# Gathered expert rows beside the first half: 2.2 per weight unit, and weights split two units ahead

## The chip, the cores and the metric

The kernel runs on one core of a Trainium2 chip. The metric is the device time of one execution in microseconds (us). TensorE (PE in the rows), VectorE (DVE), ScalarE (ACT), GpSimd (POOL) and the DMA queues of SyncE (SP) each work through their own list of instructions in order, and wait for one another by semaphores.

## What is computed

One decoder block on 512 tokens of width 1024 in f32: an adaLN-modulated RMSNorm, retention and a causal gMLP side by side, merged by sigmoid gates, one output projection, and then a PEER expert layer, which is what the change is about. Each token picks 16 experts for each of 8 heads out of 16,384 (two top-16 searches over 128 keys and a third over their sums), and needs one row of 1024 values from each of two tables for each of its 128 picks:

```
expert = k1 * PEER_N_KEYS + k2
g = jax.nn.softmax(top_s, axis=-1)
ue = expert_u[expert]                       # 128 rows of 1024 for each token
act = jax.nn.gelu(jnp.einsum('td,thkd->thk', hb, ue), approximate=False) * g
ve = expert_v[expert]
return jnp.einsum('thk,thkd->td', act, ve)
```

## The kernel before

**Tiles and stages.** The 512 tokens are four tiles of 128. Tile 0 goes through the block alone and first, and its experts are known early. The other three tiles follow together. For tiles 0 and 3 the expert layer is done by gathering; for tiles 1 and 2 by dense matmuls over all 16,384 experts, with a matrix of one-hot weights.

**Table rows.** A gathered "row" is, for one pick j, one expert's 1024 f32 values for each of the 128 tokens of a tile: an indirect DMA on POOL's queue (`gather`, L934) into a 128x1024 buffer. `consume` then does one VectorE instruction with it: for table `u` a product with the tile's activations, summed into a dot (L950); for table `v` a multiple added to an accumulator (L955). There are 512 rows: 128 of `u` and 128 of `v` for tile 0, then the same for tile 3. They are consumed in this order, in three places:
- beside the three tiles' first half, by `bg_gather`, which is called after each weight unit. A credit `cr` grows by `GB1` for each unit (by 0.6 while the seven jobs in `tq` last, that finish tile 0's search); each whole credit consumes a row and issues the next gather. Only `u` rows of tile 0 can be done here, 128 at most.
- in the query and experts-ahead phases, at fixed steps of a list that `plan` makes;
- in the final loop, where `gathers(n)` spreads whatever is left over the loop's items, in proportion to their cost.

**Weight units.** `Stream` feeds TensorE with weights in units of 128x1024. A unit is loaded by SP into a `raw` buffer (five), and, unless it is used plain, split into a high part `wh` by a ScalarE copy (L87) and a low part `wl` by a VectorE subtraction (L90). `wh` and `wl` have four buffers each. `get` returns unit k; ahead of that it issues loads as far as `ra` = 5 units, and splits as far as `sa` units (k included). Three matmuls use the parts: wh with the high activations, wl with the high, wh with the low. Gathered rows have their own buffers (two `ga`, one `gt`, later two more `gt`), and take in turns one buffer of the `wh` ring and one of the `wl` ring (`gfree += ["wh", "wl"]`); in the ring a buffer that was free longest is taken.

**The stages on which rows below are cut.** In the first half `gemm` runs 14 groups of four units: up (two groups, with gMLP mixing beside them), gate-b (two), gMLP out (two), v and g (four, with the retention's scores, products and norm beside them), gate-a (two), retention out (two). Each group ends in evictions. Then come the output projection (eight units, each raw unit scaled by a gate on VectorE, L344), the query phase (16 units, with the search for tiles 1 to 3 on VectorE), the experts-ahead phase (plain units of `uT`, L1355), and the final loop over 128 items (L1681), which loads `v`, and `uT` for the experts that weren't done ahead, splits half of the `v` units and those `uT` units, and makes the weights `aw` (L1654) and their low part `ah` (L1665) on VectorE, with the loop's gathered rows in between. Time is that of one execution from first to last instruction, and nothing is scheduled at run time: the order on each engine is that of the program.

Of the kernel before, what the change touches and what calls it, by code (L numbers as in the profile page):

```python
# [36 lines left out]
TO = 16  # L37
GSC = 2.0 ** 14
GPU = 1.4
GB1 = 1.4  # L40
VN = 2
LA = 2
PRE = 6
# [147 lines left out]
def block_kernel(ctx: ExitStack, tc: tile.TileContext, a, out, dbg=None):  # L191
# [116 lines left out]
    ws = Stream(nc, wt)  # L308
# [629 lines left out]
    def gather_all():  # L938
        while gfree and ng[0] < lim[0]:
            gather()  # L940

    def consume():
        i = ng[1]
        ng[1] += 1
        r, b = gt_t.pop(i)
        if not dropped(b):
            gfree.append(b)
        j, G = i % NJ, GT[i // (2 * NJ)]
        if i // NJ % 2 == 0:
            V.scalar_tensor_tensor(r, r, 1.0, G.h, op0=OP.mult, op1=OP.mult, accum_out=G.dots[:, j:j + 1])  # L950
            if j == NJ - 1:
                A.activation(G.dots, G.dots, AF.Gelu)
                V.tensor_tensor(G.dots, G.dots, G.g, op=OP.mult)
        else:
            V.scalar_tensor_tensor(G.acc, r, G.dots[:, j:j + 1], G.acc, op0=OP.mult, op1=OP.add)  # L955
# [21 lines left out]
    tq = []  # L977
# [34 lines left out]
    gfree += ga  # L1012
    gfree.append(t0_tile("gt"))
    gfree += ["wh", "wl"]
    ws.sa = 2
    cr = [0.0]

    def bg_gather():
        if tq:
            tq.pop(0)()  # L1020
        cr[0] = min(cr[0] + (0.6 if tq else GB1), 4.0)
        gather_all()
        while cr[0] >= 1.0 and ng[1] < ng[0]:
            cr[0] -= 1.0
            consume()
            gather_all()
# [235 lines left out]
    def xn2_tile(t):  # L1262
        rsqrt(kp, rs2[:, t:t + 1], ss2[:, t:t + 1], 1, 1.0 / D, "r2")
        V.tensor_scalar(xn2[:, t, 0:512], x2[:, t, 0:512], rs2[:, t:t + 1], None, op0=OP.mult)
        A.activation(xn2[:, t, 512:1024], x2[:, t, 512:1024], AF.Copy, scale=rs2[:, t:t + 1])
# [45 lines left out]
    for t in range(NA):  # L1311
# [6 lines left out]
        else:  # L1318
# [3 lines left out]
            ws.split(ws.ng + 2)  # L1322
            x2_tile(t + 1)
            xn2_tile(t + 1)
    ws.sa = 2
    gdrop[:] = []
    gfree += ["wh", "wl"]

# [586 lines left out]
```

## Time and profile before

| | |
|---|---|
| median of three runs | 1793.97 us (1792.15 to 1796.37) |
| profiled execution | 1793.85 us |
| its span, first to last instruction | 1791.9 us |
| instructions | 22,168 |
| busy: PE, DVE, ACT, POOL | 1590.3, 1412.2, 578.5, 750.5 us |
| bytes moved, mean rate | 601.84 MB, 336 GB/s |

The rows further down come from views of this one execution. The table by stage gives, for a stretch from A to B us: its length, then the busy time of PE, of PE's weight loads, of DVE, ACT and POOL with the number of instructions, TensorE's granted clock as a share, the mean busy share of the 16 DMA engines, and their rate. A row of waits names the engine and what it was about to write, who released it, the sum in us, the number of waits and the longest. A wait for several semaphores is put down to the one that came last. A row of the timeline gives start, duration, engine, line, operation and tiles, and in brackets the idle time ahead of it. Matmuls are pipelined and their ends are modelled, so a busy PE is not a PE at its peak.

### The profile page before, as it was taken

To read this page: it belongs to the slowest core of one execution; us is meant where nothing else is said; L and a number is where in the kernel's file an instruction comes from. 1 tells how busy PE (TensorE), PEld (TensorE's weight loads), DVE (VectorE), ACT (ScalarE), POOL (GpSimd) and SP (SyncE) were. 2 spreads that over 40 slices of the span, in tenths; PEclk is the share of its full clock that TensorE was granted. 3 is DMA by queue.
4 is the path that set the end of the run, shared out by engine and by line. 5 is a ranking of instruction groups with operands and counts; after the bars stand their busy time and mean duration, and the time that the engine had idled before them with its cause. 6 is when DMAs were issued, how large, how long until landed. Compare 5 with 4: busy or idle time off the path is not lost.

```text
span 1791.9 us, 22168 instructions
## 1 busy us (share of the span) xinstructions
PE 1590.3 (89%) x7546; PEld 1241.4 (69%) x7546; DVE 1412.2 (79%) x2862; ACT 578.5 (32%) x912; POOL 750.5 (42%) x629
## 2 busy tenths in 40 slices
PE   9999999689999798999999988877878888888886
PEld 8554578689879688988888885555555555555553
DVE  7674347977587877999999957888787888888787
ACT  7323132342233353421357642223212222221122
POOL 0111001144234131265586534557565455565563
PEclk9999999999999899999999999998999898998898
DMA  8999767378568565799999999999999999999995
GB/s 339 381 358 373 285 220 238 129 258 294 186 237 317 187 231 194 232 375 413 395 380 397 395 372 381 408 408 377 408 408 408 408 408 408 408 403 387 409 406 211
DMA packets 168497, 601.84 MB, mean 336 GB/s; under 512 B 19072, under 2 KB 19072, under 8 KB 168256
## 3 DMA queue, kind: packets, MB, share of 16 engines
q0 software_dynamic: 87888, 320.64, 46.6%
q1 hardware_dynamic: 80496, 279.78, 41.7%
q8 instruction: 60, 0.98, 0.2%
q14 instruction: 53, 0.43, 0.1%
HBM read 568.89 MB, written 31.46 MB: 335 GB/s over the span
## 4 chain that ended last, share of the span: by engine, by line
DMA 23%; DVE 15%; issue 14%; POOL 8%; PE 6%; ACT 2%; POOLq 0%; DVEq 0%; ACTq 0%
DMA gt<-in_v_dram,EB 5%; DMA gr<-in_v_dram,EB 5%; DMA gr<-in_v_dram,E 4%; POOL gr L934 4%; POOL gt L934 3%; DMA wd<-stg 3%; DMA gr<-in_u_dram,EB 2%; DMA sd<-spl 2%; DVE acc L955 2%; DVE gt L950 1%; DVE wl L90 1%; PE mm L390 1%; PE acc L1681 1%; DMA gwl<-in_v_dram,E 1%; DVE gwh L950 1%
## 5 line engine op out<-in xcount | busy, mean ns | idle before, releaser
L90 DVE TENSOR_TENSOR wl<-raw,wh 128x1024 fp32r<-128x1024 f32 x208 | 255.0, 1228 | 73.0 <-ACT wh L87 66.1
L1355 PE MATMUL mm<-h2F,raw 128*128 128x256 f32 (+1 forms) x1296 | 283.5, 380 | 0.3 <-ACT stg L1549 0.3
L1355 PEld LDWEIGHTS mm<-h2F,raw 128*128 128x128 f32 x1296 | 244.0, 192 | 32.9 <-ACT stg L1549 0.4
L1681 PE MATMUL acc<-wh,ah 128*128 128x512 f32 x512 | 197.2, 491 | 77.8 <-DVE ah L1665 65.1
L87 ACT CAST wh<-raw 128x1024 fp32r<-128x1024 f32 x208 | 215.7, 1045 | 130.1 <-DVE gwh L950 31.9
L1681 PE MATMUL acc<-raw,aw 128*128 128x512 f32 x512 | 235.1, 601 | 1.0 <-DVE aw L1654 1.0
L1681 PEld LDWEIGHTS acc<-wh,ah 128*128 128x128 f32 x512 | 109.5, 221 | 127.5 <-DVE ah L1665 71.6
L1662 ACT CAST ah<-aw 128x256 fp32r<-128x256 f32 x64 | 26.0, 406 | 458.2 <-DVE aw L1654 443.9
L1681 PEld LDWEIGHTS acc<-raw,aw 128*128 128x128 f32 x512 | 98.3, 195 | 98.8 <-issue 92.4
L1681 PE MATMUL acc<-wl,ah 128*128 128x512 f32 x256 | 94.9, 455 | 39.8 <-DVE wl L90 39.7
L1347 PE MATMUL mm<-h2H,wl 128*128 128x256 f32 x384 | 112.6, 293 | 10.8 <-DVE wl L90 10.8
L1345 PE MATMUL mm<-h2H,wh 128*128 128x256 f32 x384 | 120.8, 315 | 1.4 <-ACT wh L87 1.4
L950 DVE SCALAR_TENSOR_TENSOR gr<-gr,h2B 128x1024 f32<-128x1024 f32 x74 | 89.7, 1222 | 32.3 <-DMA gr<-in_u_dram,EB 31.2
L955 DVE SCALAR_TENSOR_TENSOR accB<-gr,dB,accB 128x1024 f32<-128x1024 f32 x72 | 92.4, 1284 | 27.7 <-DMA gr<-in_v_dram,EB 25.9
L1346 PE MATMUL mm<-h2L,wh 128*128 128x256 f32 x384 | 111.9, 292 | 0.0
L934 POOL DMA_INDIRECT gr<-in_v_dram,EB x72 | 87.3, 1213 | 56.7 <-DVE accB L955 33.8
L934 POOL DMA_INDIRECT gr<-in_u_dram,EB x74 | 85.4, 1154 | 60.8 <-DVE gr L950 47.3
L934 POOL DMA_INDIRECT ga<-in_u_dram,E x30 | 42.0, 1399 | 162.0 <-DVE ga L950 109.0
L416 PE MATMUL mm<-raw,h 128*128 128x512 f32 x224 | 102.2, 598 | 3.8 <-DMA raw<-in_w_in_dram 3.8
L934 POOL DMA_INDIRECT gt<-in_v_dram,EB x56 | 77.3, 1381 | 60.5 <-DVE accB L955 43.3
L934 POOL DMA_INDIRECT gt<-in_u_dram,E x40 | 55.0, 1376 | 111.7 <-DVE gt L950 42.1
L1681 PEld LDWEIGHTS acc<-wl,ah 128*128 128x128 f32 x256 | 53.4, 217 | 63.1 <-DVE wl L90 50.3
(447 smaller groups left out, 3738.8 us busy)
## 6 DMA issues: line engine op xcount, KB each, us to landing
raw<-in_uT_dram SPq DMA_DIRECT2D x128, 512.0 KB
raw<-in_v_dram SPq DMA_DIRECT2D x128, 512.0 KB
raw<-in_w_in_dram SPq DMA_DIRECT2D x112, 512.0 KB
raw<-in_w_q_dram SPq DMA_DIRECT2D x32, 512.0 KB
wd<-stg POOLq DMA_DIRECT2D x8, 2048.0 KB
wqb<-wd SPq DMA_DIRECT2D x32, 512.0 KB
ada<-in_w_ada_dram POOLq DMA_DIRECT2D x28, 512.0 KB
sd<-spl POOLq DMA_DIRECT2D x40, 256.0 KB
```

What stands on the lines that cost most here:

```text
L87: self.nc.scalar.copy(h, r)
L90: self.nc.vector.tensor_tensor(l, r, h.bitcast(F32), op=OP.subtract)
L416: T.matmul(ps, s[:, d, :], r[:, dd * 512:(dd + 1) * 512], start=(d == 0), stop=(d == ND - 1))
L934: P.indirect_dma_start(out=r, out_offset=None, in_=a[tab], in_offset=bass.IndirectOffsetOnAxis(ap=G.E[:, j:j + 1], axis=0))
L950: V.scalar_tensor_tensor(r, r, 1.0, G.h, op0=OP.mult, op1=OP.mult, accum_out=G.dots[:, j:j + 1])
L955: V.scalar_tensor_tensor(G.acc, r, G.dots[:, j:j + 1], G.acc, op0=OP.mult, op1=OP.add)
L1345: T.matmul(ps[:, p:q], h[:, d, :], h2H[:, d, cs], start=(d == 0), stop=False)
L1346: T.matmul(ps[:, p:q], h[:, d, :], h2L[:, d, cs], start=False, stop=False)
L1347: T.matmul(ps[:, p:q], l[:, d, :], h2H[:, d, cs], start=False, stop=(d == ND - 1))
L1355: T.matmul(ps[:, p:q], r[:, d, :], h2F[:, d, p:q], start=(d == 0), stop=(d == ND - 1))
L1662: A.copy(hl[:, 0], w)
L1681: T.matmul(accs[2 * t + e], s_, y[:, e * 512:(e + 1) * 512], start=s0_, stop=s1_)
```

## The change

```diff
-GB1 = 1.4
+GB1 = 2.2
@@ block_kernel, ahead of the three tiles' first half
     gfree += ["wh", "wl"]
-    ws.sa = 2
     cr = [0.0]
 
     def bg_gather():
         if tq:
             tq.pop(0)()
-        cr[0] = min(cr[0] + (0.6 if tq else GB1), 4.0)
+        cr[0] = min(cr[0] + (0.5 if tq else GB1), 4.0)
         gather_all()
@@ block_kernel, behind the output projection
             xn2_tile(t + 1)
-    ws.sa = 2
+    ws.sa = 3
     gdrop[:] = []
```

In the first half `sa` keeps the 3 that it had before, so at unit k the split of k+2 is issued, where it was that of k+1; in the query phase it is set to 3 as well. The credit of a unit is 2.2 rows, and 0.5 while `tq` lasts. Nothing else is edited; lines behind the removed one are one lower in the changed kernel. What moves, at three places:

VectorE in the second gMLP-out group, four units and its eviction (L1078), before. L90 makes a unit's `wl`; L950 consumes a `u` row:

```order
L90 TENSOR_TENSOR wl<-raw,wh 128x1024
L950 SCALAR_TENSOR_TENSOR gwh,d_1824<-gwh,h_1683 128x1024
L90 TENSOR_TENSOR wl<-raw,wh 128x1024
L950 SCALAR_TENSOR_TENSOR gwl,d_1824<-gwl,h_1683 128x1024
L90 TENSOR_TENSOR wl<-raw,wh 128x1024
L950 SCALAR_TENSOR_TENSOR ga,d_1824<-ga,h_1683 128x1024 x2
L90 TENSOR_TENSOR wl<-raw,wh 128x1024
L950 SCALAR_TENSOR_TENSOR gt,d_1824<-gt,h_1683 128x1024
L1078 TENSOR_TENSOR brb<-mm,brb 128x384 x4
```

The same group in the changed kernel, from the eviction of the first group (now L1077) to the middle of the fourth unit:

```order
L1077 TENSOR_TENSOR brb<-mm,brb 128x384 x4
L90 TENSOR_TENSOR wl<-raw,wh 128x1024
L950 SCALAR_TENSOR_TENSOR gwh,d_1824<-gwh,h_1683 128x1024
L950 SCALAR_TENSOR_TENSOR gwl,d_1824<-gwl,h_1683 128x1024
L950 SCALAR_TENSOR_TENSOR ga,d_1824<-ga,h_1683 128x1024
L90 TENSOR_TENSOR wl<-raw,wh 128x1024
L950 SCALAR_TENSOR_TENSOR ga,d_1824<-ga,h_1683 128x1024
L950 SCALAR_TENSOR_TENSOR gt,d_1824<-gt,h_1683 128x1024
L90 TENSOR_TENSOR wl<-raw,wh 128x1024
L950 SCALAR_TENSOR_TENSOR gwh,d_1824<-gwh,h_1683 128x1024
L950 SCALAR_TENSOR_TENSOR gwl,d_1824<-gwl,h_1683 128x1024
```

Between two splits one or two rows stood, and now there are two or three.

VectorE at the end of the first half, before, with the numbers of the tiles. L344 scales a raw unit of the projection; 4465 is its first unit, 4503 its second:

```order
L344 TENSOR_TENSOR raw_4503<-raw_4503,gates_98 128x1024
L90 TENSOR_TENSOR wl_4571<-raw_4465,wh_4570 128x1024
L950 SCALAR_TENSOR_TENSOR ga_2228,d0_1824<-ga_2228,h20_1683 128x1024
L1200 TENSOR_TENSOR mg_4600<-mm_4471,sga_4156 128x384
...
L1203 TENSOR_TENSOR mL_4304<-mg_4615,mH_4303 128x384
L950 SCALAR_TENSOR_TENSOR ga_2229,d0_1824<-ga_2229,h20_1683 128x1024
L1230 MEMSET acc0_4634 128x1024
L344 TENSOR_TENSOR raw_4535<-raw_4535,gates_98 128x1024
L90 TENSOR_TENSOR wl_4652<-raw_4503,wh_4651 128x1024
```

The same place in the changed kernel, where 4557, 4594 and 4628 are the projection's first three units:

```order
L90 TENSOR_TENSOR wl_4631<-raw_4557,wh_4630 128x1024
L950 SCALAR_TENSOR_TENSOR gt_4390,d0_1824<-gt_4390,h20_1683 128x1024
L950 SCALAR_TENSOR_TENSOR ga_2228,d0_1824<-ga_2228,h20_1683 128x1024
L344 TENSOR_TENSOR raw_4628<-raw_4628,gates_98 128x1024
L90 TENSOR_TENSOR wl_4665<-raw_4594,wh_4664 128x1024
...
L1202 TENSOR_TENSOR mL_4388<-mg_4713,mH_4387 128x384
L1229 MEMSET acc0_4731 128x1024
L344 TENSOR_TENSOR raw_4662<-raw_4662,gates_98 128x1024
L90 TENSOR_TENSOR wl_4749<-raw_4628,wh_4748 128x1024
```

The second unit's `wl` stood behind the last evictions (L1200 to L1203), and stands ahead of them now.

VectorE in the loop, around one item with its `uT` matmuls (`aw<-gs`) and the next, before:

```order
L1654 TENSOR_TENSOR aw<-gs,wqb 128x256
L950 SCALAR_TENSOR_TENSOR gt,dB<-gt,h2B 128x1024 x2
L950 SCALAR_TENSOR_TENSOR gr,dB<-gr,h2B 128x1024 x2
L1665 TENSOR_TENSOR ah<-aw,ah 128x256
L90 TENSOR_TENSOR wl<-raw,wh 128x1024
```

And in the changed kernel:

```order
L1653 TENSOR_TENSOR aw<-gs,wqb 128x256
L950 SCALAR_TENSOR_TENSOR gt,dB<-gt,h2B 128x1024
L950 SCALAR_TENSOR_TENSOR gr,dB<-gr,h2B 128x1024 x2
L1664 TENSOR_TENSOR ah<-aw,ah 128x256
L90 TENSOR_TENSOR wl<-raw,wh 128x1024
```

Four rows stood between `aw` and `ah` of such an item, and three do now.

## Rows read from the trace of the kernel before

**Rows 1.** The page's 40 slices: busy share of the DMA engines.

```profile
DMA  8999767378568565799999999999999999999995
```

**Rows 2.** Table by stage, up and gate-b to projection, query, experts-ahead, loop.

```profile
291.80:395.00 103.20, 80.98 (x442) 77.93 (x443) 87.79 (x280) 36.25 (x58) 29.86 (x22) 0.93 0.56 194
395.00:428.10 33.10, 33.10 (x193) 33.10 (x192) 25.93 (x37) 9.75 (x10) 17.53 (x13) 1.00 0.92 328
428.10:524.00 95.90, 91.80 (x394) 74.87 (x393) 66.23 (x126) 27.71 (x35) 34.84 (x25) 0.96 0.64 221
524.00:561.70 37.70, 36.58 (x218) 35.72 (x217) 27.34 (x40) 16.84 (x25) 14.16 (x11) 1.00 0.71 238
561.70:599.60 37.90, 35.21 (x194) 34.57 (x193) 31.68 (x46) 10.61 (x14) 15.57 (x11) 0.95 0.78 294
599.60:643.00 43.40, 36.41 (x153) 29.32 (x152) 29.18 (x47) 16.97 (x26) 2.74 (x5) 0.88 0.44 151
643.00:760.00 117.00, 108.23 (x623) 103.30 (x622) 101.38 (x399) 52.71 (x110) 34.89 (x32) 0.97 0.68 234
760.00:1060.00 300.00, 291.51 (x1717) 257.33 (x1716) 284.21 (x652) 141.35 (x207) 178.19 (x150) 0.99 1.01 389
...
1085.00:1770.00 685.00, 565.08 (x2253) 385.05 (x2251) 568.39 (x733) 149.50 (x220) 393.96 (x311) 0.91 1.02 400
```

**Rows 3.** DMA view of the final loop: rate in 40 slices, bytes.

```profile
GB/s 340 409 408 409 409 409 407 408 323 412 409 407 408 408 409 408 407 408 409 410 406 407 407 410 405 408 408 409 399 409 406 408 382 381 409 407 404 408 408 321
DMA packets 78131, 274.30 MB, mean 400 GB/s; under 512 B 8683, under 2 KB 8683, under 8 KB 78095
```

**Rows 4.** VectorE's largest waits in the loop, 1085 to 1770 us.

```profile
DVE gr L950 <- DMA gr<-in_u_dram,EB: 31.2, 34, 3.4
DVE accB L955 <- DMA gr<-in_v_dram,EB: 25.9, 29, 1.3
```

**Rows 5.** TensorE's largest waits in the loop, 1085 to 1770 us.

```profile
PE acc L1681 <- DVE ah L1665: 65.1, 15, 8.2
PE acc L1681 <- DVE wl L90: 39.7, 22, 5.3
```

**Rows 6.** DMA view of the first half, 291.8 to 599.6 us.

```profile
DMA packets 19787, 72.11 MB, mean 234 GB/s; under 512 B 2224, under 2 KB 2224, under 8 KB 19768
```

**Rows 7.** Line 934, 291.8 to 643 us: duration min/median/max ns; who waited.

```profile
L934 POOL DMA_INDIRECT ga<-in_u_dram,E x30: 932/1674/1977, 294.9 to 574.0; - x30
...
  DVE gt L950: 0.4, 1
```

**Rows 8.** TensorE's waits, 291.8 to 643 us.

```profile
PE mm L390 <- DVE wl L90: 15.5, 9, 3.5
PE mm L388 <- ACT wh L87: 11.2, 5, 4.4
PE mm L384 <- DVE wl L90: 7.4, 2, 4.1
PE mm L383 <- ACT wh L87: 3.7, 1, 3.7
```

**Rows 9.** VectorE's timeline in the second gate-b group.

```profile
382.10 1.22 DVE L950 SCALAR_TENSOR_TENSOR gt<-gt,h 128x1024 f32<-128x1024 f32 x1
...
383.25 1.22 DVE L90 TENSOR_TENSOR wl<-raw,wh 128x1024 fp32r<-128x1024 f32 x1
```

**Rows 10.** ScalarE's waits ahead of a copy, 291.8 to 643 us.

```profile
ACT wh L87 <- DVE gwh L950: 30.8, 8, 6.1
...
ACT wh L87 <- PE mm L385: 23.5, 6, 7.4
```

**Rows 11.** The page's groups: ScalarE's copy of a unit.

```profile
L87 ACT CAST wh<-raw 128x1024 fp32r<-128x1024 f32 x208 | 215.7, 1045 | 130.1 <-DVE gwh L950 31.9
```

**Rows 12.** ScalarE's timeline: a table load.

```profile
371.46 1.28 ACT L1071 ACT_TABLE_LOAD   x1
```

**Rows 13.** A wait of POOL for a slot, 291.8 to 643 us.

```profile
POOL gwl L934 <- PE mm L390: 2.5, 3, 1.9
```

## The prediction

> **What bounds the kernel now.** The slices of the profile come first [rows 1]: from the 18th slice, about 760 us, the DMA engines stand at nine tenths or more in every slice but the last; ahead of that they mostly do not. The table by stage [rows 2] says the same in numbers, with the engines beside it. In the final loop (1085 to 1770 us) the DMA share is 1.02 at 400 GB/s, while TensorE is busy for 565.1 of 685 us and VectorE for 568.4. The loop's rate stands flat at 399 to 412 GB/s in 35 of its 40 slices [rows 3], as a resource at its limit does. The waits agree: VectorE's two largest are for gathered rows to land, 31.2 and 25.9 us [rows 4], and TensorE waits for what VectorE makes behind those rows, `ah` for 65.1 us and `wl` for 39.7 us [rows 5]. So in the loop a transfer ends last, and each table row in it costs its bytes.
>
> The three-tile first half (291.8 to 599.6 us) is another regime. 72.11 MB move there at 234 GB/s [rows 6]; the rows come early, since up to the end of the projection VectorE waited once for one, 0.4 us [rows 7]; and TensorE waits for the split of a weight unit, 15.5 + 11.2 + 7.4 + 3.7 = 37.8 us in 17 waits, the projection's included [rows 8]. Between the two, from 760 to 1060 us, TensorE (291.5 of 300 us), VectorE (284.2) and DMA (1.01) are all full [rows 2].
>
> **The change, part by part.** Counted on VectorE in the order of the instructions, 74 rows stand ahead of the projection in the kernel before and 113 in the changed one; from there to the loop both have 128; in the loop 310 become 271. So 39 rows move from the loop into the first half, and none is added.
>
> *Rows taken out of the loop.* A row is 128 lines of 1024 f32, 0.524 MB; 39 are 20.45 MB. The loop needs 685 / 274.30 = 2.497 us for a MB [rows 3], so 51.1 us. VectorE is relieved by 39 x 1.15 us [rows 9] = 45 of its 568.4 us and does not take over. TensorE keeps its 565.1 us; of the 119.9 us that it idles, 104.8 are the two waits on VectorE [rows 5], so it could do the loop in some 580, below the 634 that DMA would then need. Ends: 51 if DMA stays the only limit; 45 if the 5 of 40 slices under 395 GB/s [rows 3] give nothing; 25 if the loop keeps half. In the last, TensorE can't be busy for the 565/634 = 89% that the full gain asks for; but behind the same splits it reaches 35.2/37.9 = 93% from 561.7 to 599.6 us [rows 2], so I take the middle of the two near ends: **-48 us**.
>
> *Rows put into the first half.* Beside another VectorE instruction a row takes 1.15 us (from 382.10 to 383.25 us) [rows 9], and I take as much for the other passes over a 128x1024 tile, the `wl` and the scaling of `w_out`. 39 rows are 44.9 us of VectorE in a stretch, the projection included, in which it is busy 268 of 351 us [rows 2]. By group, with the rows counted in the order: up and gate-b 87.8 + 8 x 1.15 = 97.0 us in 103.2; gMLP out 25.9 + 6.9 = 32.8 in 33.1; v and g 66.2 + 13.8 = 80.0 in 95.9; gate-a 27.3 + 8.1 = 35.4 in 37.7; retention out 31.7 + 6.9, and another split with its scaling that moves in from the projection, 2.3, = 40.9 in 37.9. Only the last is over: +3 us. In bytes gMLP out has 328 GB/s x 33.1 us = 10.9 MB; 6 rows make it 14.0 MB, and at the loop's 400 GB/s these take 35.0 us: +2 us.
>
> The rows of the loop show that this core's transfers hold 400 GB/s [rows 2]. The Trainium skill ("DMA: Bandwidth & Descriptors", Specifications) gives an HBM limit of about 358 GB/s for a core. By an estimate from that figure the 14.0 MB would take 39.1 us, and this group would cost +6 instead of +2; the trace differs, and the measurement decides.
>
> *Splits one unit earlier.* With `sa` = 3 the split of unit k+2 stands ahead of the table rows and evictions of unit k. That adds no instruction, but a wait: while a gathered row holds a `wh` slot, three slots are left for units, so ScalarE's copy for k+2 waits for TensorE's end of k-1, VectorE's `wl` waits behind it, and the rows of unit k behind that. Such waits stand in the trace of before too: 23.5 us of ScalarE for TensorE, 30.8 us for a row that held the slot [rows 10]. TensorE still has k and k+1 split then, each 33.1/8 = 4.1 us [rows 2], against 1.05 us for the copy [rows 11] and 1.15 us for the `wl`. I cost the wait at nothing; with that cover gone it is 2.2 us a unit. SP's queue gains by it, since its loads wait for `wl` to free a raw slot; POOL's gathers wait for slots as they do now.
> What it gives: at the start of the projection TensorE waits 3.7 us for a copy [rows 8] and some 3.3 of the 7.4 us for a `wl`, of a unit whose split stood behind the evictions and now stands ahead of them: -4. Elsewhere the longest waits were 4.4 and 4.1 us [rows 8]; these two joints can give 8, and I take half, -4, since VectorE is fuller. Against that, rows now come in twos and threes between splits on three nearly full engines: +6, an estimate of 0.5 us for each of the 12 groups of four units from gate-b on. Sum for first half and projection: +3 + 2 - 4 - 4 + 6 = **+3 us**. Ends: -13 (every group at its largest need, of VectorE, DMA or TensorE: 97 + 35 + 91.8 + 36.6 + 40.9 + 36.4 = 338 against 351) and +45 (no row covered).
>
> *Query phase* (643 to 760 us): the same number of rows, splits a unit earlier. TensorE idles 8.8 us there and VectorE is busy 101.4 of 117 us [rows 2]. Row 128, where the dots get their gelu, comes into this phase, and a ScalarE table load of 1.28 us with it [rows 12]. Ends -7 and +4, taken **-2 us**.
>
> Sum: -48 + 3 - 2 = -47. The profiled execution took 1793.85 us (span 1791.9 and 1.95 around it), 0.12 under the median of the runs shown; 1793.85 - 47 = 1746.9, so **1747 us**.
>
> **Rivals.**
> *A, the first half gives half of it back.* VectorE, at 99% of gMLP out and over 100% of retention out, can't do rows and splits in time, and TensorE waits for `wl` more than now: +25 there instead of +3, 1769 us. For it: the sums by group; against it: 83 us of idle VectorE in the stretch.
> *B, the loop keeps half.* TensorE's waits for `ah` are waits for an order as much as for bytes, as the rows stand between `aw` and `ah`: -25 instead of -48, 1770 us. For it: 15 waits of up to 8.2 us [rows 5]; against it: the flat rate.
> *C, the lookahead pays in full.* First half -13, query phase -7, loop -51: 1723 us.
> *D, slower: the ring of slots.* The gather into `wh` takes the slot of unit k and waits on POOL until TensorE has ended k; POOL works in order, so the gathers behind it wait too, and the row is wanted five rows later. There are 113/5 = 23 such rounds. If in each VectorE waits for a whole unit, 4.1 us, that is 94 us: 1841 us. It decides from 47/23 = 2.0 us a round. Against it: five rows at 2.2 a unit are 2.3 units, 12 us at the present 308/56 = 5.5 us a unit, and such waits of POOL for TensorE (L390) are 2.5 us in three now [rows 13].
> *E, POOL's descriptors.* A gather holds POOL for 0.93 to 1.98 us, median 1.67, in the first half [rows 7]. 113 at 1.98 are 224 of 308 us. Were each held for another row's 1.22 us [rows 9], they were 362 us, 54 too many: 1801 us. The Trainium skill ("SBUF — State Buffer", Summary: rules for kernel authors) has a rule of this kind: descriptor generation on GpSimd starves while VectorE runs in a 2x or 4x mode. The spread of the gathers agrees with some holding; no row here shows which VectorE instruction does it.
> *F, nothing gained*: the rows move, but every stage keeps its length, 1794 us.
>
> **How the numbers follow.** Forecast (1737 to 1757) 0.60, A 0.14, B 0.10, C 0.08, D 0.03, E 0.02, F 0.03. The range from 1733 to 1770 leaves out most of C, D, E, F and the far half of A and B, about 2 in 10. A measurement of this kernel tells some 0.2%, 3.6 us, from no change. Faster: forecast, A, B and C, 0.92; slower: D and E, 0.05; same: F, 0.03.
>
> **What would show it.** The loop should shorten to about 637 us with its DMA share still at 1.0 and 400 GB/s; a share under 0.95 there speaks for B. From the first up unit to the projection's end it should stay within 351 ± 10 us with VectorE near 313 us busy; longer by over 15 with TensorE waiting for `wl` is A, with VectorE waiting for rows D, with POOL never idle E. The waits for splits (37.8 us) should fall, most plainly at the projection's start. From 760 to 1060 us it should keep its 300 us; I'd be wrong if that lengthens.

## The result and the profile after

The changed kernel takes 1764.13 us (median of four runs, 1760.54 to 1765.71) against 1793.25 us (1792.15 to 1796.37): a ratio of 0.9832, 95% interval 0.9812 to 0.9852. That is faster by 29 us, where 47 were forecast; 1747 was 17 us too low, and the range of 1733 to 1770 holds the time. The profiled execution took 1765.71 us, with a span of 1763.7.

The table by stage, cut at the same places of the program as [rows 2], shows where the time went. The columns are length, busy time and instructions of PE, PE's weight loads, DVE, ACT and POOL, granted clock, DMA share and GB/s; the six rows are up and gate-b, gMLP out, v and g, gate-a, retention out, projection:

```profile
293.20:396.40 103.20, 83.22 (x442) 80.68 (x443) 92.94 (x289) 36.99 (x58) 35.82 (x26) 0.87 0.61 210
396.40:430.50 34.10, 33.83 (x193) 33.20 (x193) 30.82 (x47) 7.81 (x9) 23.74 (x18) 1.00 1.01 387
430.50:531.30 100.80, 93.40 (x393) 75.07 (x393) 80.37 (x154) 27.68 (x35) 52.58 (x40) 0.97 0.79 275
531.30:570.40 39.10, 36.32 (x219) 35.87 (x218) 36.24 (x56) 18.90 (x28) 27.67 (x19) 1.00 0.96 352
570.40:615.20 44.80, 36.49 (x193) 34.99 (x192) 37.38 (x55) 10.56 (x13) 22.78 (x18) 0.89 0.82 310
615.20:662.10 46.90, 38.45 (x152) 30.43 (x152) 33.86 (x57) 16.14 (x25) 7.07 (x8) 0.85 0.56 189
```

The same of the changed kernel for four long stretches: first half and projection; from there to the query phase's last unit; experts-ahead; and the loop from its first to its last matmul into the accumulators:

```profile
293.20:662.10 368.90, 321.72 (x1584) 290.24 (x1585) 311.61 (x653) 118.09 (x166) 169.66 (x125) 0.92 0.75 269
662.10:765.50 103.40, 95.83 (x545) 91.99 (x544) 85.59 (x312) 46.36 (x94) 26.22 (x26) 0.93 0.64 217
765.50:1081.90 316.40, 306.42 (x1776) 269.08 (x1775) 300.19 (x697) 145.10 (x222) 184.12 (x153) 0.98 0.99 380
1109.30:1755.30 646.00, 565.27 (x2288) 381.65 (x2288) 534.67 (x718) 158.52 (x230) 341.58 (x274) 0.94 1.00 395
```

The first, third and fourth of these in the kernel before:

```profile
291.80:643.10 351.30, 314.19 (x1584) 285.58 (x1585) 268.24 (x575) 118.22 (x166) 114.70 (x86) 0.95 0.64 224
745.80:1055.40 309.60, 303.25 (x1777) 267.94 (x1775) 294.77 (x727) 145.92 (x219) 179.04 (x151) 0.99 1.00 385
1082.10:1783.80 701.70, 579.85 (x2288) 394.25 (x2288) 579.98 (x757) 156.84 (x232) 396.91 (x313) 0.90 1.00 393
```

So the loop lost 701.7 - 646.0 = 55.7 us, more than the 48 forecast, at the same DMA share and rate. First half and projection grew by 368.9 - 351.3 = 17.6, where 3 were forecast; from the projection to the loop it grew by 8.2 (439.0 to 447.2), where -2 was forecast; the start lies 1.4 us later. -55.7 + 17.6 + 8.2 + 1.4 and 0.3 at the end make the -28.2 us between the spans. Of the 17.6 us, retention out has 6.9, v and g 4.9, the projection 3.5.

TensorE's waits in first half and projection of the changed kernel; the columns are as in [rows 8], the sum in us, the number, the longest:

```profile
PE mm L388 <- ACT wh L87: 12.9, 3, 7.3
PE mm L384 <- DVE wl L90: 8.1, 4, 2.9
PE mm L390 <- DVE wl L90: 7.9, 6, 3.4
PE mm L388 <- DVE mx L1038: 7.9, 1, 7.9
PE mm L383 <- ACT wh L87: 4.2, 1, 4.2
PE mm L388 <- DVE zL L1164: 2.8, 1, 2.8
PE mm L383 <- DVE mg L1199: 2.2, 1, 2.2
```

The waits for splits fell only from 37.8 us [rows 8] to 33.1 (those for `wl` from 22.9 to 16.0), and waits for evictions that VectorE makes (`mx`, `zL`, `mg`) have come in: 12.9 us, none of which stood there before. The longest wait for a split, 7.3 us, lies in the middle of retention out, and the timeline shows how it comes about. VectorE first (start, length, engine, line, tiles; idle time ahead in brackets):

```profile
587.83 1.22 DVE L950 SCALAR_TENSOR_TENSOR gwl<-gwl,h 128x1024 f32<-128x1024 f32 x1
...
590.12 1.22 DVE L950 SCALAR_TENSOR_TENSOR gt<-gt,h 128x1024 f32<-128x1024 f32 x1
...
591.26 1.22 DVE L90 TENSOR_TENSOR wl<-raw,wh 128x1024 fp32r<-128x1024 f32 x1
...
593.54 1.22 DVE L950 SCALAR_TENSOR_TENSOR ga<-ga,h 128x1024 f32<-128x1024 f32 x1
...
594.69 0.55 DVE L1199 TENSOR_TENSOR mg<-mm,sga 128x384 f32<-128x384 f32 x1
```

Then ScalarE and TensorE:

```profile
595.87 0.52 ACT L1201 CAST mH<-mg 128x384 fp32r<-128x384 f32 x1 [8.27 <-DVE mg L1200]
...
602.47 0.51 ACT L1201 CAST mH<-mg 128x384 fp32r<-128x384 f32 x1 [1.69 <-DVE mg L1200]
602.88 1.99 ACT L87 CAST wh<-raw 128x1024 fp32r<-128x1024 f32 x2
...
603.98 0.69 PE L388 MATMUL mm<-zH,wh 128*128 128x384 f32 x1 [7.33 <-ACT wh L87]
```

VectorE is busy throughout, with five rows (587.83, 588.97, 590.12, 592.40 and 593.54) and a split in 7 us. The four evictions (`mg`) stand behind them; ScalarE's copies of the evictions (`mH`) wait for those, 8.27 us for the first; and the copies of the next units (`wh`), which need nothing of the evictions, stand behind the `mH` on ScalarE. Both units that were split ahead are used up by then.

### The profile page after: what moved, and what is told of

Read it like the earlier page. It is cut to its first block, busy times and chain, and to the rows that moved or that the text cites. A ratio compares the mean times of both kernels' runs of the same rounds, so it can differ in the third digit from the quotient of the medians.

```text
span 1763.7 us, 22139 instructions
## 1 busy us (share of the span) xinstructions
PE 1589.2 (90%) x7546; PEld 1237.1 (70%) x7546; DVE 1414.4 (80%) x2862; ACT 581.4 (33%) x914; POOL 750.5 (43%) x629
## 4 chain that ended last, share of the span: by engine, by line
DVE 25%; DMA 24%; PE 23%; issue 15%; POOL 9%; ACT 3%; SPq 0%; POOLq 0%; DVEq 0%; ACTq 0%
DMA gr<-in_v_dram,EB 10%; PE mm L416 6%; DVE acc L955 5%; POOL gr L934 4%; DMA gt<-in_v_dram,EB 3%; POOL gt L934 3%; DVE wl L90 3%; PE mm L384 2%; PE mm L385 2%; PE mm L383 2%; PE acc L1680 2%; DMA sd<-spl 1%; DMA gt<-in_v_dram,E 1%; DMA gwh<-in_u_dram,E 1%; DVE gt L950 1%
## 5 line engine op out<-in xcount | busy, mean ns | idle before, releaser
L90 DVE TENSOR_TENSOR wl<-raw,wh 128x1024 fp32r<-128x1024 f32 x208 | 259.0, 1249 | 68.2 <-ACT wh L87 66.1
L1680 PE MATMUL acc<-wh,ah 128*128 128x512 f32 x512 | 185.8, 465 | 48.8 <-DVE ah L1664 36.3
L1680 PEld LDWEIGHTS acc<-wh,ah 128*128 128x128 f32 x512 | 103.0, 208 | 98.8 <-DVE ah L1664 43.7
L934 POOL DMA_INDIRECT gr<-in_v_dram,EB x74 | 94.2, 1273 | 82.6 <-DVE accB L955 69.5
L934 POOL DMA_INDIRECT ga<-in_u_dram,E x44 | 65.7, 1493 | 132.4 <-DVE ga L950 75.2
L934 POOL DMA_INDIRECT gt<-in_v_dram,E x46 | 63.2, 1374 | 108.8 <-DVE acc L955 51.2
L950 DVE SCALAR_TENSOR_TENSOR gr<-gr,h2B 128x1024 f32<-128x1024 f32 x72 | 86.9, 1221 | 22.0 <-DMA gr<-in_u_dram,EB 22.0
L934 POOL DMA_INDIRECT gt<-in_u_dram,EB x56 | 69.3, 1238 | 65.7 <-DVE gt L950 53.5
L934 POOL DMA_INDIRECT gt<-in_v_dram,EB x54 | 65.2, 1208 | 56.5 <-DVE accB L955 40.1
## 6 DMA issues: line engine op xcount, KB each, us to landing
wd<-stg POOLq DMA_DIRECT2D x8, 2048.0 KB, 17.1
```

What stands on the lines that cost most here:

```text
L90: self.nc.vector.tensor_tensor(l, r, h.bitcast(F32), op=OP.subtract)
L934: P.indirect_dma_start(out=r, out_offset=None, in_=a[tab], in_offset=bass.IndirectOffsetOnAxis(ap=G.E[:, j:j + 1], axis=0))
L1680: T.matmul(accs[2 * t + e], s_, y[:, e * 512:(e + 1) * 512], start=s0_, stop=s1_)
```

## The experiments

Two theories stood at first. **A**: the rows fill VectorE in the first half, whatever the splits do. **S**: the splits two units ahead, which bring a split and rows ahead of evictions, make the first half long. For each kernel the table gives the rows consumed ahead of the projection's end, `sa` in the first half, the length of first half with projection and of the loop (from first to last matmul, profiled execution), the median, and the ratio to the kernel before on the same chip.

| kernel | rows | `sa` | first half, projection | loop | median us | ratio (95%) |
|---|---|---|---|---|---|---|
| before | 74 | 2 | 351.3 | 701.7 | 1793.3 | 1 |
| changed | 113 | 3 | 368.9 | 646.0 | 1764.1 | 0.9832 (0.9812 to 0.9852) |
| splits_alone | 74 | 3 | 336.9 | 698.3 | 1779.9 | 0.9942 (0.9928 to 0.9957) |
| rows_alone | 113 | 2 | 378.5 | 645.3 | 1769.8 | 0.9878 (0.9860 to 0.9895) |
| query_sa2 | 113 | 3 | 370.9 | 646.5 | 1761.9 | 0.9833 (0.9817 to 0.9848) |
| narrow39 | 113 | 3 | 352.8 | 646.3 | 1746.5 | 0.9745 (0.9729 to 0.9760) |
| thin39 | 113 | 3 | 350.6 | 645.7 | 1741.0 | 0.9700 (0.9678 to 0.9721) |
| evict_first | 113 | 3 | 368.8 | 646.0 | 1765.4 | 0.9846 (0.9830 to 0.9863) |
| evict_first_128 | 128 | 3 | 387.4 | 631.0 | 1772.2 | 0.9877 (0.9857 to 0.9898) |
| no_slots | 113 | 3 | 424.1 | 645.2 | 1813.9 | 1.0110 (1.0092 to 1.0129) |
| raw_slot | 113 | 3 | 364.6 | 647.1 | 1761.9 | 0.9834 (0.9814 to 0.9854) |
| six_bufs | 113 | 3 | 361.6 | 646.0 | 1757.6 | 0.9823 (0.9801 to 0.9844) |
| rate18 | 93 | 3 | 343.8 | 673.4 | 1763.9 | 0.9849 (0.9827 to 0.9871) |
| six_ret18 | 109 | 3 | 359.2 | 654.0 | 1762.2 | 0.9818 (0.9792 to 0.9844) |

**The two parts apart.** rows_alone keeps `sa` = 2 in both places:

```diff
-GB1 = 1.4
+GB1 = 2.2
...
-        cr[0] = min(cr[0] + (0.6 if tq else GB1), 4.0)
+        cr[0] = min(cr[0] + (0.5 if tq else GB1), 4.0)
```

> The change with its rows alone: 2.2 rows per unit (0.5 while `tq` lasts), but `sa` = 2 in both places as before. The same 39 rows move, so on either theory the loop should take about 646 us, as in the changed kernel, against 702 before. Theory A (the rows fill VectorE in the first half, whatever the splits do): first half and projection stay long, 365 to 375 us against 351 before and 369 in the changed kernel, and the time is 1760 to 1772 us. Theory S (the splits two units ahead, which put a split and rows ahead of the evictions, make the first half long): first half and projection fall to about 355 us and the time is about 1750 us.

splits_alone is the other half:

```diff
     gfree += ["wh", "wl"]
-    ws.sa = 2
     cr = [0.0]
...
-    ws.sa = 2
+    ws.sa = 3
     gdrop[:] = []
```

> The change with its splits alone: `sa` = 3 in both places, 1.4 rows per unit (0.6 while `tq` lasts) as before. The loop should stay at about 702 us. Theory A: the splits cost nothing; first half and projection take 343 to 353 us (351 before), and the time is 1784 to 1795 us. Theory S: the splits stand ahead of evictions that TensorE waits for; first half and projection take 360 us or more, and the time is 1803 us or more.

First half and projection, of rows_alone and of splits_alone:

```profile
289.50:668.00 378.50, 326.39 (x1586) 294.89 (x1587) 312.63 (x654) 118.42 (x166) 169.79 (x125) 0.91 0.72 262
```

```profile
289.80:626.70 336.90, 309.79 (x1586) 282.41 (x1587) 267.29 (x576) 118.31 (x166) 111.28 (x86) 0.96 0.65 233
```

S falls: the splits alone shorten the stretch by 14.4 us, and with the many rows by 9.6 (378.5 to 368.9). Of A it stands that the rows make the stretch long: 39 of them lengthen it by 27.2 us behind splits one ahead, and by 32.0 behind splits two ahead. Both lengths missed A's forecasts, though: rows_alone's 378.5 lies above 365 to 375, and splits_alone's 336.9 below 343 to 353, as A held the splits to be worth nothing. TensorE's waits in rows_alone are of one kind, for splits:

```profile
PE mm L390 <- DVE wl L90: 18.2, 12, 4.4
PE mm L384 <- DVE wl L90: 14.5, 5, 6.6
PE mm L388 <- ACT wh L87: 13.9, 5, 7.6
PE mm L383 <- ACT wh L87: 6.1, 1, 6.1
```

That is 52.7 us against 37.8 [rows 8], with 32.7 for `wl`. In splits_alone those for `wl` are 9.8:

```profile
PE mm L390 <- DVE wl L90: 6.4, 5, 3.4
...
PE mm L384 <- DVE wl L90: 3.4, 1, 3.4
```

The loop is the same with either `sa`, 645.3 and 646.0, and with the splits alone it is 698.3 against 701.7, so its gain is nearly all the rows'.

**The query phase.** query_sa2 is the changed kernel with the old value behind the projection:

```diff
-    ws.sa = 3
+    ws.sa = 2
     gdrop[:] = []
```

> The changed kernel with `sa` set back to 2 behind the output projection; the first half is untouched and should take 369 us, the loop 646. In the changed kernel the stretch from the projection's end to the query phase's end took 103.4 us against 102.7 before, so on theory A `sa` = 3 is worth nothing there: 1762 to 1766 us. Theory S: it costs there too (the first 20.1 us of it were 15.8 before), and the time is 1758 to 1761 us.

From the projection's end to the query phase's end it took 104.7 us, against 103.4 with 3 there: the joint in between is shorter (16.9 against 20.1 us) and the phase longer (87.8 against 83.3). The time is the same within the intervals. `sa` = 3 is worth nothing there, and nothing is lost by it.

**What of a row costs.** narrow39 gathers the same rows, but the instruction on VectorE for 39 of them is 64 columns wide, so that the other columns are left out of their dots:

```diff
+            w = 64 if i < 113 and (i * 39) // 113 != ((i + 1) * 39) // 113 else 1024
-            V.scalar_tensor_tensor(r, r, 1.0, G.h, op0=OP.mult, op1=OP.mult, accum_out=G.dots[:, j:j + 1])
+            V.scalar_tensor_tensor(r[:, 0:w], r[:, 0:w], 1.0, G.h[:, 0:w], op0=OP.mult, op1=OP.mult, accum_out=G.dots[:, j:j + 1])
```

> The changed kernel, where 39 of the 113 first-half rows, evenly spread, are gathered whole but consumed by an instruction over 64 instead of 1024 columns (so their dots lack the other columns). VectorE is relieved of 39 x about 1.08 = 42 us; gathers, buffers and bytes stay. Theory A with VectorE as the cause: first half and projection come back to 348 to 355 us, the time to 1744 to 1751 us. If instead the gathers (their bytes, their slots in the rings, POOL) make the first half long: it stays at 365 to 370 us and the time at 1760 to 1766 us.

thin39 cuts the gathers of these 39 as well:

```diff
-        P.indirect_dma_start(out=r, out_offset=None, in_=a[tab],
+        w = 64 if i < 113 and (i * 39) // 113 != ((i + 1) * 39) // 113 else 1024
+        P.indirect_dma_start(out=r[:, 0:w], out_offset=None, in_=a[tab] if w == 1024 else a[tab].rearrange("n (k c) -> (n k) c", c=64),
```

> As narrow39, and the gathers of the same 39 rows are cut to 64 columns (a sixteenth of the bytes; as many lines, instructions, buffers and slots), so their dots come from wrong and fewer values. narrow39 took 352.8 us for first half and projection, 16 us more than the 336.9 of the splits alone, with VectorE waiting 34 us for rows to land. Theory B (these 16 us are bytes: transfers at the limit make rows land late): it falls to 337 to 342 us and the time to 1731 to 1736 us. Theory R (they are slots and order, not bytes): it stays at 350 to 354 us and the time at 1744 to 1748 us.

First half and projection, of narrow39 and of thin39:

```profile
290.00:642.80 352.80, 314.66 (x1586) 286.65 (x1587) 274.42 (x654) 117.69 (x166) 148.73 (x125) 0.94 0.76 281
```

```profile
292.40:643.00 350.60, 313.52 (x1585) 285.98 (x1586) 273.51 (x653) 118.17 (x166) 155.21 (x125) 0.95 0.67 228
```

So the 32.0 us that 39 rows cost behind the splits two ahead come apart: VectorE's time, 368.9 - 352.8 = 16.1 us, with VectorE busy for 37 us less; the bytes, 352.8 - 350.6 = 2.2 us, with 19 MB less; and 350.6 - 336.9 = 13.7 us that stay. Some work is in these still: VectorE is busy for 273.51 us in thin39 and 267.29 in splits_alone. Each length is that of one execution, and the changed kernel and query_sa2, which are the same up to the projection's end, differ by 2.0 us, so the 2.2 us can't be told from nothing. narrow39 came out as the first forecast had it. The length of thin39 is that of its second forecast, so the bytes don't make up what stayed; its time, 1741.0 us, lies between the two. VectorE's waits for rows in thin39 point to what may make it up:

```profile
DVE ga L952 <- DMA ga<-in_u_dram,E: 21.4, 11, 5.2
DVE gwh L952 <- DMA gwh<-in_u_dram,E: 3.6, 5, 1.4
DVE gwl L952 <- DMA gwl<-in_u_dram,E: 3.2, 3, 1.8
```

VectorE waits 28 us for these rows to land, against 14 us for all rows in the changed kernel and none in splits_alone: with less to do it wants its rows sooner than five buffers bring them.

**Where the rows stand.** The timeline above suggested that a row costs where it stands ahead of an eviction. In evict_first the rows of a group's fourth unit stand behind it:

```diff
-            bg[0]()
+            if u < 3:
+                bg[0]()
         for ps, b in banks:
             evict(b, ps)
+        bg[0]()
```

> The changed kernel, where the table rows of a group's fourth unit stand behind the group's evictions instead of ahead of them; number of rows and everything else stay. Theory Q (rows cost because they stand in VectorE's queue ahead of evictions, and ScalarE's copies for the next units queue behind the copies of those evictions): the one wait of 7.3 us in retention out, the 4.2 us at the projection's start and some of the waits in v and g go, first half and projection fall from 369 to 352 to 360 us, the time to 1746 to 1755 us. Theory L (only VectorE's sum of work and the landing of rows count, wherever the rows stand): first half stays at 366 to 370 us and the time at 1760 to 1766 us.

The stretch takes 368.8 us, to a tenth of what it was, and that theory falls. Waits of TensorE in evict_first:

```profile
PE mm L390 <- DVE wl L90: 13.7, 9, 3.9
PE mm L384 <- DVE wl L90: 11.3, 4, 5.6
...
PE mm L388 <- ACT wh L87: 7.1, 4, 5.0
PE mm L383 <- ACT wh L87: 4.8, 1, 4.8
```

The waits for ScalarE's copies fell from 17.1 to 11.9 us, and those for `wl` rose from 16.0 to 25.0: the wait changed its name. The chain in the timeline is how VectorE's lack of time reached TensorE at that place, not why it lacked.

**How many rows.** evict_first_128 is evict_first with a credit of 2.7; rate18 is the changed kernel with 1.8:

```diff
-GB1 = 2.2
+GB1 = 2.7
```

```diff
-GB1 = 2.2
+GB1 = 1.8
```

> As evict_first, with a credit of 2.7 rows per unit, by which all 128 u rows that tile 0 has stand ahead of the projection's end instead of 113: 15 more rows out of the loop. The loop should be shorter by 15 x 0.524 MB x 2.5 us/MB = 20 us. By the price that the 39 rows had behind the three-ahead splits (32 us, 0.83 us a row) the first half takes 12 us more, and the time is 8 us under evict_first; if the last rows cost their whole 1.15 to 1.3 us, the two are the same within 3 us; if VectorE is full and each costs more than its transfer in the loop, it is slower.

> The changed kernel with 1.8 rows per unit: 93 rows ahead of the projection's end instead of 113 (74 with 1.4). The loop should take 20 x 1.43 = 29 us more than 646, as each of the 39 rows gave 55.7/39 = 1.43. If a row's cost in the first half is the same for each (32 us for 39, with splits three ahead): first half and projection take 337 + 19 x 0.83 = 352 us and the time is 1775 us, between that of the splits alone (1780) and the changed kernel (1764). If the cost lies in the last rows (VectorE over its fill in a few groups): 340 to 346 us and 1763 to 1769 us, no worse than the changed kernel.

A row's cost is far from constant. Between 74 and 93 rows (splits_alone to rate18) the first half grows by 6.9 us, 0.36 a row; between 93 and 113 (rate18 to the changed kernel) by 25.1, 1.26 a row; between 113 and 128 (the two evict_first) by 18.6, 1.24 a row. The loop gives 24.9/19 = 1.31, 27.4/20 = 1.37 and 15.0/15 = 1.00. So the first 19 rows give nearly 1 us each, the next 20 give nothing, and the last 15 seem to lose (evict_first_128 takes 6.9 us more than evict_first by the medians, but the intervals of the two ratios just overlap); rate18 and the changed kernel take the same time, as the second of rate18's forecasts had it. First half and projection, of rate18 and of evict_first_128:

```profile
290.90:634.70 343.80, 312.00 (x1584) 282.88 (x1585) 288.79 (x613) 117.43 (x166) 137.52 (x105) 0.96 0.71 258
```

```profile
292.60:680.00 387.40, 325.03 (x1585) 287.80 (x1586) 330.99 (x684) 119.85 (x168) 188.47 (x137) 0.94 0.75 272
```

VectorE's busy share of the stretch is 267.29/336.9 = 79% in splits_alone, 84% in rate18, 84% in the changed kernel and 85% with 128 rows. It rose with the first rows and has stood since: behind that a row lengthens the stretch by its own duration and a little more. By stage, rows consumed and length in us, counted by the starts of the rows in the trace:

| stage | splits_alone | rate18 | changed |
|---|---|---|---|
| up and gate-b | 17, 98.2 | 18, 98.5 | 22, 103.0 |
| gMLP out | 11, 33.4 | 17, 33.4 | 17, 34.3 |
| v and g | 21, 88.9 | 27, 92.3 | 35, 100.4 |
| gate-a | 13, 36.2 | 16, 36.3 | 18, 39.3 |
| retention out | 9, 34.9 | 11, 35.9 | 17, 44.8 |
| projection | 3, 45.0 | 4, 47.2 | 4, 47.1 |

The borders of this table lie up to 0.5 us ahead of those of the rows by stage, and a row that starts at a border moves with it: by the later borders gMLP out has 15 rows in rate18 and retention out 16 in the changed kernel. In gMLP out the rows that rate18 adds cost nothing at all, although it is the stage fullest of transfers. In retention out the last five or six cost 8.9 us. rate18's row for that stage has VectorE busy for 30.36 us:

```profile
551.60:587.60 36.00, 34.17 (x194) 33.08 (x192) 30.36 (x45) 10.26 (x13) 14.87 (x11) 1.00 0.80 309
```

Five or six more rows of 1.15 us [rows 9] would make 36.1 to 37.3 in 36.0.

**The buffers.** no_slots takes the `wh` and `wl` slots from the rows of the first half; raw_slot gives them one of the five `raw` buffers instead of one of the four `wh`; six_bufs gives them one `raw` more. In this order:

```diff
-    gfree += ["wh", "wl"]
     cr = [0.0]
```

```diff
-    gfree += ["wh", "wl"]
+    gfree += ["raw", "wl"]
...
-            gdrop += ga + ["wh", "wl"]
+            gdrop += ga + ["raw", "wl"]
```

```diff
-    gfree += ["wh", "wl"]
+    gfree += ["wh", "wl", "raw"]
...
-            gdrop += ga + ["wh", "wl"]
+            gdrop += ga + ["wh", "wl", "raw"]
```

> The changed kernel, where the rows of the first half use only their own buffers (two `ga`, one `gt`) and no slot of the `wh` and `wl` rings. ScalarE's waits for a row that held a slot (51.5 us in twelve) go. Theory R (those slots delay splits for which TensorE waits): first half and projection fall to 355 to 362 us, 1749 to 1757 us in all. Theory L (rows land late: VectorE's waits for rows were 13 us): with three buffers instead of five each row is issued later, VectorE waits for many of the 113 rows, 0.5 to 1 us each, and the first half takes 385 us or more, the time 1780 us or more.

> The changed kernel, where the rows of the first half take one buffer of the `raw` ring (five of them) instead of one of the `wh` ring; two `ga`, one `gt` and one `wl` stay, so there are five row buffers as before. ScalarE's waits for a row that held a `wh` slot (51.5 us in twelve) go; loads of weights are asked for a unit later. Theory R (a row in the `wh` ring holds up splits that TensorE waits for): first half and projection fall from 369 to 355 to 362 us and the time to 1750 to 1757 us. Theory V (VectorE has too much to do between the waits that its order sets, whatever the slots): 366 to 372 us, 1761 to 1767 us. If loads then come late, TensorE and ScalarE wait for `raw` from DMA and it is over 375 us.

> The changed kernel with a sixth row buffer in the first half: one of the `raw` ring beside `ga`, `ga`, `gt`, `wh` and `wl`. Rows are then asked for earlier. VectorE's waits for rows to land (13 us in the first half of the changed kernel, 28 with 39 rows cut thin) should go. If late rows are the 14 us that stayed with thin39: first half and projection fall to 355 to 362 us, the time to 1750 to 1757 us. Theory V: 366 to 372 us and 1761 to 1767 us.

With three buffers the stretch takes 424.1 us, as theory L had it, and VectorE's largest wait in no_slots is for rows to land:

```profile
DVE ga L950 <- DMA ga<-in_u_dram,E: 61.0, 32, 4.4
```

In the changed kernel all of VectorE's waits for rows are 14 us. That a row lands in time is a matter of buffers here. ScalarE's waits for a row in a `wh` slot are gone in raw_slot, and waits for loads have come instead, the largest of them:

```profile
ACT wh L87 <- DMA raw<-in_w_in_dram: 23.0, 7, 6.8
```

The stretch is 4.3 us shorter with raw_slot, outside both of its forecasts, and 7.3 with six_bufs, at the edge of the better one. VectorE's waits for rows did not go with a sixth buffer: they fell from 14 to 9 us. And the 7.3 us flatter it, since the profiled execution of six_bufs is the fastest of its five and that of the changed kernel the slowest of its four. The medians are 2 and 6.5 us under the changed kernel's; the ratios, 0.9834 and 0.9823 against 0.9832, don't tell them apart from it.

six_ret18 is six_bufs with a credit of 1.8 in retention out:

```diff
+    rate[0] = 1.8
     for g in range(2):
         gemm("tr", zH, zL, ev_ret(g))
```

> six_bufs (1757.6 us), with the credit lowered from 2.2 to 1.8 rows per unit in the retention-out groups alone: 109 rows ahead of the projection's end instead of 113. In the changed kernel and in six_bufs retention out consumes 17 and 18 rows in 44.8 and 45.8 us, with 1.8 everywhere 11 rows in 35.9 us, with 2.2 and plain lists of buffers never under 41 us. If the cost of the last rows sits in that stage (1.5 us a row, as its evictions are VectorE's work and ScalarE's copies for the next units stand behind them): retention out falls by 6 to 10 us, the loop grows by 4 x 1.4 = 5.5 us, and the time is 1753 to 1757 us. If what is lowered there comes back as waits elsewhere (the projection behind it, whose 47 us are 45 with the splits alone): it is 1758 to 1763 us.

Retention out falls by 3.2 us (45.8 to 42.6), not by 6 to 10, and the loop grows by 8.0 where 5.5 were expected. The time is that of the second forecast, though not for its reason, since the projection did not grow (45.5 to 44.2 us). No version that does the whole work was measurably faster than the changed kernel.

## Why the prediction came out as it did

**The range held, and the loop's mechanism did, but two terms were mis-sized.** 1764 lies outside the likeliest case (1737 to 1757), and nearest to rival A (1769). The runs show A's mechanism in part: VectorE's time makes half of what the rows cost, but its sign, more waits of TensorE for `wl`, shows where the splits stay the same (22.9 to 32.7 us with splits one ahead, 9.8 to 16.0 with two), while from the kernel before to the changed one they fell (22.9 to 16.0). That the range held was in part luck: the loop gave 7.7 us more than forecast, and without them the time would have been 1772, past the range's end.

**The loop: -48 taken, -55.7 measured; -51.1 by bytes.** A transfer ended last there, as argued from [rows 3 to 5]: share and rate stayed, and TensorE's waits for VectorE shrank with the rows. In the loop of the changed kernel:

```profile
PE acc L1680 <- DVE ah L1664: 36.3, 16, 4.2
PE acc L1680 <- DVE wl L90: 31.5, 20, 3.4
```

Against splits_alone, whose loop holds the same rows as that of before, the gain is 52.3 us, the price by bytes; the nine kernels with 113 rows lie between 645.2 and 647.1. Choosing the middle of the near ends, out of doubt that TensorE could be busy 89% of the time, was a step too far: it is busy for 565.27 of 646.0 us, 88%. Rival B is out.

**The first half: +3 taken, +17.6 measured. This is the step that failed**, in *Rows put into the first half*. The rows were priced at 3 + 2 + 6 = +11 us and cost 27 to 32; the splits at -8 and gave -9.6 to -14.4. The count of VectorE's work was right (313 us forecast, 311.61 measured), and it named the right stage, since only retention out was over its length. The error was to set each group's sum of work against its length, and to let a group cost nothing while the sum fitted. v and g, at 80.0 of 95.9 us by that sum, grew by 4.9. An engine that works in order can't use the time in which it waits: VectorE's waits for ScalarE's `z` (9.2 us) and for TensorE's scores (8.0 us, one wait) lie in v and g in the changed kernel, and it is 80% busy there and no more:

```profile
DVE st L1129 <- ACT z L1126: 9.2, 4, 3.0
DVE PT L1099 <- PE mm L1098: 8.0, 1, 8.0
```

So by rate18, the one point between, the cost set in where VectorE was 84% busy over the whole stretch, not at 100%: 0.36 us a row up to there, 1.26 behind. And it was VectorE's time for half of it only (16.1 of 32.0 us). Of the rest, 13.7 us stay when 39 rows lose nearly all their work and bytes. The waits for rows in thin39 speak for rows that land late, and so does the shorter stretch of six_bufs, but no run shows how much that is: this part stays open.

**gMLP out's bytes: +2 taken, +1.0 measured** at 387 GB/s. By an estimate from the Trainium skill's limit of about 358 GB/s for a core ("DMA: Bandwidth & Descriptors", Specifications), which the same page (Bandwidth) gives as the share of each core when both cores of an HBM domain stream, it would have been +6; the trace does not agree with that limit for the one core that runs here.

**The splits' cover held for the splits, and failed at evictions.** The waits for splits were to fall, most plainly at the projection's start: there the prediction lists 3.7 and 3.3 us and takes 4 for them without a reason. In the changed kernel TensorE waits 4.2 us for a copy, 2.1 for a `wl` and 2.2 for `mg` there, and the wait for the copy ends 16.3 us into the projection instead of 7.9. So it moved to a later unit, and this joint gave nothing. Of the 14.4 us that the splits alone gave, 6.6 came in v and g, where TensorE is busy for 89.2 of 89.3 us in splits_alone, against 91.80 of 95.90 [rows 2], and 4.8 in up and gate-b. A wait that no term held came with the splits: 7.9 us for `mx` in gate-b, 6.7 in splits_alone, which neither the kernel before nor rows_alone has.

**From the projection to the loop: -2 taken, +8.2 measured.** The query phase did what was said (86.9 to 83.3 us), and the joint ahead of it took 4.3 back. Experts-ahead, which was to keep its length, took 6.8 us more, with the DMA share at 0.99 and 380 GB/s against 385; the prediction had named that as a sign of being wrong, and no term held it. It is 4.9 longer in splits_alone, whose rows there are those of before, and 6.5 longer in rows_alone, whose splits are those of before. So either half of the change lengthens it alone, at nearly the same bytes (119.2 MB before, 120.3 in the changed kernel). Why is open.

**Rivals.** D and E didn't come: VectorE waited 14 us for rows in all of the stretch, not 94, and POOL is busy for 169.66 of 368.9 us. C's value for the splits (-13 in the first half) is what splits_alone measured, -14.4; it was the rows that took it back.

## What to carry to other kernels

Work that is moved beside other work starts to cost before its engine is full: price it by what the engine waits for in that stretch as well as by what it does, and measure the cost at two amounts, since it bends. Where two edits come together, try each alone: here the smaller-looking one (splits a unit earlier) gave 10 to 14 us in its stretch, and the last half of the larger one gave nothing. And a wait that a timeline explains fully may only be the place where a lack shows: when it is taken away there and the stretch keeps its length, look for the resource and not for the order.

## What the hardware showed

A wait of TensorE costs again through its clock. The three stretches are of retention out in the changed kernel, ahead of the wait of 7.33 us, from its end on, and a microsecond behind that:

```profile
590.00:596.60 6.60, 6.46 (x36) 5.86 (x34) 5.98 (x12) 0.52 (x1) 5.22 (x4) 1.00 1.02 408
604.00:608.60 4.60, 4.35 (x12) 3.84 (x13) 4.60 (x7) 0.87 (x1) 1.68 (x1) 0.50 0.38 118
609.60:614.90 5.30, 5.30 (x33) 5.30 (x32) 5.30 (x8) 1.29 (x2) 1.68 (x1) 1.00 0.63 190
```

The granted clock falls from 1.00 to 0.50, the lower of its two levels (1.2 GHz), and a matmul of 128x384 takes 0.52 instead of 0.33 us until it rises again. The Trainium skill ("TensorE: Matmul & The Clock Gate", Part 1) states that an idle TensorE is gated to the lower of these levels; the trace agrees. No term of the sum held this. TensorE's busy time in first half and projection was 309.79 us in splits_alone and 321.72 in the changed kernel, for the same matmuls: of the 32.0 us that the 39 rows cost, 11.9 are longer busy time, with a mean granted clock of 0.92 instead of 0.96, and 20.1 are idle time. The clock is shown as the cause at the one wait above; for the whole stretch it is inferred from these means.
